# Four tiles instead of three for each part of the divided weights

## The chip, the cores and the metric

The kernel runs on one core of one Trainium2 chip. The metric is the device time of one execution in microseconds (us), lower is better.

## The reference

The reference is one block of a trunk on x of 512 tokens by 1024 features, float32 throughout. With u = rms_norm(x):

```
fa, fb, fc, fd, fg = split(u @ w_in)
branches = rwkv7_mix(fa), gla_mix(fb), mlstm_mix(fc), ssd_mix(fd)      # each [512, 512]
gates    = sigmoid(fg)                                                # four of [512, 1024]
merged   = sum_i gates[i] * (branches[i] @ branch_proj[i])
h = x + merged @ w_out
gate, val = split(causal_dwconv(rms_norm(h) @ ffn_up, 3 taps))        # 2 x 2816
h = h + (silu(gate) * val) @ ffn_down
return rms_norm(h)
```

The four mixers are recurrences over the tokens (RWKV7, gated linear attention, mLSTM, state space), computed here in chunks. `ssd_mix` matters below. For each of four blocks of 128 tokens and each of eight heads it forms exp(min(a_t - a_s, 0)) under a causal mask, multiplies it by the product of C and B, and applies that 128 by 128 matrix to the values.

## The kernel before, in words

**The dense work.** Every large matrix is read from memory in halves of 128 by 512 floats (256 KB). `split_h` (lines 220 to 228) handles one half: SP issues the load into a `raw` tile (line 222, three of them), ACT rounds it into `hi` (line 225), and DVE, or POOL for some, writes the rest, raw - hi, into `lo` (line 226). Both come from `w_tiles` (lines 217 and 218), a ring of three tiles for `hi` and three for `lo`. A product is then three matmuls (`mm3`, lines 234 to 237): hi by hi, lo by hi, hi by lo. A half feeds 12 matmuls in `fm` (512 tokens wide, called wide below) and 24 in `tm` and `fm_halves` (256 wide, called narrow below). A `hi` tile is free again when the last matmul that reads it is done; the next cast into it waits for that.

**The branches** interleave with it. The RWKV part runs in two halves. Each half solves a triangular system by 62 dependent instructions on DVE (lines 600 and 602 in turns), sends the result out and back by DMA, and goes on at line 629; its last matmuls are at lines 728 and 736. `conv4` (line 907 three times, line 910) and the GLA preparation (line 805) work on finished dense products and so free their PSUM banks, of which the dense products have three.

**The state space part** (`ssd`, named the SSD stage below: from the first half's line 728 to the last of lines 1056 and 1062). For each block b = 0 to 3: SP broadcasts a row of decays into a `sab` tile of 512 KB (line 1019, two tiles, so the third transfer waits for the matmuls of the first block), DVE and POOL take half of the subtractions each (line 1041, eight per block), ACT takes the exponential (line 1042), POOL applies the mask (line 1043), DVE multiplies by the product (line 1052), and PE applies the result (line 1056). POOL has small steps between these (lines 1039, 1057, 1064, 1073).

**The tail.** After the last branch come w_out, the norm, and the up projection. Its first two columns (`first`, line 1239) run by halves of tokens. For the second of these columns the second half of the weights has two tiles of its own, `wxh` and `wxl`, from a pool that lives until line 1240. The FFN loop (lines 1268 to 1273) and the down projection follow; line 1265 is their convolution.

**What sets the order.** The program is written once, and a scheduler of the framework then orders the instructions of every engine by a simulated timeline, with priorities from a table of numbers. Each engine runs its list strictly in order. The number of tiles in a ring is an input to that simulation.

Of the kernel before, what the change touches and what calls it, by code (L numbers as in the profile page):

```python
# [10 lines left out]
F32R = mybir.dt.float32r  # L11
# [5 lines left out]
P = 128  # L17
# [143 lines left out]
def kernel(ctx: ExitStack, tc: tile.TileContext, A, out):  # L161
# [25 lines left out]
    wp = ctx.enter_context(tc.tile_pool(name="wp", bufs=1))  # L187
# [7 lines left out]
    def pd():  # L195
        return dense[0].tile([P, T], F32, tag="d", name="psd")
# [18 lines left out]
        return pf[lo:hi, PF_AT[name] + i:PF_AT[name] + i + 1]  # L215

    def w_tiles():
        return (wp.tile([P, 512], F32R, tag="hi", name="hi", bufs=3), wp.tile([P, 512], F32R, tag="lo", name="lo", bufs=3))

    def split_h(src, h, tiles=None, eng=V):  # L220
        raw = wp.tile([P, 512], F32, tag="raw", name="raw", bufs=NRAW)
        nc.sync.dma_start(raw, src[:, 512 * h:512 * h + 512])
        hi, lo = tiles or w_tiles()
        with tc.high_priority(Q["split"]):
            S.copy(hi, raw)  # L225
            eng.tensor_tensor(lo, raw, hi.bitcast(F32), op=ALU.subtract)  # L226
        return hi, lo
# [3 lines left out]
    def split_w(src, tiles=(None, None), eng=V):  # L231
        return [split_h(src, h, tiles[h], G if (pl[0] >> h) & 1 else eng) for h in range(2)]

    def mm3(ps, lh, ll, rh, rl, first, last):
        PE.matmul(ps, lh, rh, start=first, stop=False)  # L235
        PE.matmul(ps, lh, rl, start=False, stop=False)  # L236
        PE.matmul(ps, ll, rh, start=False, stop=last)  # L237
# [36 lines left out]
    def fm_halves(jobs, eng=V):  # L274
        ws = [split_w(src, tiles, eng) for src, tiles in jobs]
        pss = [pd() for _ in jobs]
        for h in range(2):
            ts = slice(256 * h, 256 * h + 256)
            for w, ps in zip(ws, pss):
                for k in range(KD):  # L280
                    hi, lo = w[k // 4]
                    ks = slice((k % 4) * P, (k % 4 + 1) * P)
                    mm3(ps[:, ts], hi[:, ks], lo[:, ks], uh[:, k, ts], ul[:, k, ts], k == 0, k == KD - 1)
        return pss
# [924 lines left out]
    nc.sync.dma_start(gb2, A["gvec"][D:2 * D].partition_broadcast(P))  # L1209
    gb3 = hp.tile([P, D], F32, name="gb3")  # L1210
    nc.sync.dma_start(gb3, A["gvec"][2 * D:3 * D].partition_broadcast(P))
    hw_ctx = ExitStack()
    hw = hw_ctx.enter_context(tc.tile_pool(name="hw", bufs=1, side="right", reuse_waits="tile"))
    wx = [hw.tile([P, 512], F32R, name=n) for n in ("wxh", "wxl")]
    hx = ExitStack()
    np_ = hx.enter_context(tc.tile_pool(name="nq", bufs=1, side="right", reuse_waits="tile"))

# [18 lines left out]
        norm_T(h2[:, b], gb2, b, np_, uh, ul, 1, [pr_, pm])  # L1236
    tap("h2", h2)
    hx.close()
    first = fm_halves([(A["up"][0], (None, None)), (A["up"][1], (None, (wx[0], wx[1])))])
    hw_ctx.close()  # L1240
    wo_ctx.close()
    mo_ctx.close()
    ps_ctx.close()
# [91 lines left out]
```

## Time and profile before

| | |
|---|---|
| median of 3 runs | 1195.45 us (1193.54 to 1199.78) |
| the profiled execution | 1195.54 us |
| its span, first to last instruction | 1193.7 us |
| mean granted TensorE clock | 0.984 |
| busy PE / DVE / ACT / POOL | 1143.7 / 651.6 / 444.4 / 331.4 us |
| chain that ended last | PE 74%, DVE 11%, DMA 7%, issue 4% |

The profiled execution is 1.8 us longer than its span and 0.1 us above the median. The busy time of PE counts overlapping matmuls once. The chain is followed back from the last instruction to whatever released each step.

### The profile page before, as it was taken

How to read it: one execution, taken by the hardware profiler on the slowest of the kernel's cores; microseconds unless marked ns; L12 is line 12 of the kernel's file. 1: busy time of each engine (PE TensorE's matmuls, PEld its weight loads, DVE VectorE, ACT ScalarE, POOL GpSimd, SP SyncE). 2: the span in 40 equal slices, each digit the busy share in tenths (PEclk: the TensorE clock that was granted, in tenths of full speed). 3: DMA queues.
4: the chain of work that ended last, by engine and by line, in shares of the span. 5: the costliest groups of instructions: out<-in, count | busy, mean ns of one | idle time of the engine just before them, and what ended most of it. 6: DMA issues, size and time to landing. Idle time of an engine off the chain costs nothing.

```text
span 1193.7 us, 17895 instructions
## 1 busy us (share of the span) xinstructions
PE 1143.7 (96%) x6881; PEld 928.9 (78%) x6881; DVE 651.6 (55%) x1090; ACT 444.4 (37%) x820; POOL 331.4 (28%) x287
## 2 busy tenths in 40 slices
PE   5999989999999999989999999999999999999997
PEld 4887868777788767778777777778788888888886
DVE  5258796453576365793235653554665666652323
ACT  4355234332333432232124343432444444442323
POOL 3104012230285543331114543620212222220100
PEclk9999989999998999999999999999999999999999
DMA  5222322322341322332224523561232223222322
GB/s 198 65 98 64 88 61 70 103 78 79 105 98 53 98 80 67 93 83 91 68 84 150 160 88 115 184 201 38 89 101 96 96 96 99 97 97 97 97 97 107
DMA packets 79886, 117.30 MB, mean 98 GB/s; under 512 B 22660, under 2 KB 27172, under 8 KB 79800
## 3 DMA queue, kind: packets, MB, share of 16 engines
q1 hardware_dynamic: 79224, 115.11, 30.6%
q8 instruction: 54, 0.88, 0.3%
q10 hardware_dynamic: 576, 1.05, 0.2%
q14 instruction: 32, 0.26, 0.1%
HBM read 107.93 MB, written 8.19 MB: 97 GB/s over the span
## 4 chain that ended last, share of the span: by engine, by line
PE 74%; DVE 11%; DMA 7%; issue 4%; ACT 2%; POOL 1%; SPq 1%; POOLq 0%; DVEq 0%; ACTq 0%
PE psd L235 17%; PE psd L236 16%; PE psd L237 16%; PE psd L1282 3%; PE psd L1283 3%; PE psd L1284 3%; DVE Mi L602 2%; DVE Mt L600 2%; DMA sab<-ad 2%; DVE lo L226 1%; PE psr L676 1%; PE psd L331 1%; PE psd L330 1%; DMA raw<-in_wo_dram 1%; PE psd L332 1%
## 5 line engine op out<-in xcount | busy, mean ns | idle before, releaser
L226 DVE TENSOR_TENSOR lo<-raw,hi 128x512 fp32r<-128x512 f32 x280 | 229.0, 819 | 312.0 <-ACT hi L225 300.6
L225 ACT CAST hi<-raw 128x512 fp32r<-128x512 f32 x322 | 199.6, 620 | 485.7 <-PE psd L236 300.9
L235 PE MATMUL psd<-uh,hi 128*128 128x512 f32 (+1 forms) x912 | 359.9, 395 | 11.5 <-DVE w L907 4.8
L237 PE MATMUL psd<-uh,lo 128*128 128x512 f32 (+1 forms) x912 | 357.6, 393 | 4.5 <-DVE lo L226 4.1
L236 PE MATMUL psd<-ul,hi 128*128 128x512 f32 (+1 forms) x912 | 356.2, 391 | 0.2 <-DVE ul L252 0.2
L235 PEld LDWEIGHTS psd<-uh,hi 128*128 128x128 f32 x912 | 172.2, 189 | 53.0 <-ACT hi L225 6.2
L237 PEld LDWEIGHTS psd<-uh,lo 128*128 128x128 f32 x912 | 172.2, 189 | 44.8 <-DVE lo L226 5.6
L236 PEld LDWEIGHTS psd<-ul,hi 128*128 128x128 f32 x912 | 172.3, 189 | 36.8 <-issue 2.6
L226 POOL TENSOR_TENSOR lo<-raw,hi 128x512 fp32r<-128x512 f32 x42 | 56.9, 1356 | 194.2 <-ACT hi L225 157.5
L1271 POOL TENSOR_TENSOR y<-y 128x512 f32<-128x512 f32 x22 | 28.3, 1288 | 174.0 <-DVE y L1265 160.1
L1265 DVE SCALAR_TENSOR_TENSOR y<-psd,pf,y 128x510 f32<-128x510 f32 x88 | 65.9, 750 | 2.7
L1284 PE MATMUL psd<-hi,al 128*128 128x512 f32 x164 | 63.8, 389 | 0.0
L1283 PE MATMUL psd<-lo,ah 128*128 128x512 f32 x164 | 63.8, 389 | 0.0
L331 PE MATMUL psd<-lo,uh 128*128 128x256 f32 x192 | 57.1, 298 | 1.0 <-DVE lo L226 1.0
L1282 PE MATMUL psd<-hi,ah 128*128 128x512 f32 x164 | 57.3, 389 | 0.0
L332 PE MATMUL psd<-hi,ul 128*128 128x256 f32 x192 | 56.3, 294 | 0.0
L330 PE MATMUL psd<-hi,uh 128*128 128x256 f32 x192 | 55.8, 292 | 0.0
L331 PEld LDWEIGHTS psd<-lo,uh 128*128 128x128 f32 x192 | 37.8, 197 | 5.2 <-issue 3.3
L332 PEld LDWEIGHTS psd<-hi,ul 128*128 128x128 f32 x192 | 37.9, 197 | 1.3 <-issue 1.0
L330 PEld LDWEIGHTS psd<-hi,uh 128*128 128x128 f32 x192 | 37.7, 197 | 1.6 <-issue 1.2
L1284 PEld LDWEIGHTS psd<-hi,al 128*128 128x128 f32 x164 | 30.8, 188 | 6.5
L1282 PEld LDWEIGHTS psd<-hi,ah 128*128 128x128 f32 x164 | 30.8, 188 | 6.4
(418 smaller groups left out, 1696.5 us busy)
## 6 DMA issues: line engine op xcount, KB each, us to landing
raw<-in_wfm_dram SPq DMA_DIRECT2D x140, 256.0 KB, 2.6
raw<-in_up_dram SPq DMA_DIRECT2D x88, 256.0 KB, 2.5
raw<-in_dn_dram SPq DMA_DIRECT2D x44, 256.0 KB, 2.5
raw<-in_bp_dram SPq DMA_DIRECT2D x32, 256.0 KB, 2.7
raw<-in_wtm_dram SPq DMA_DIRECT2D x24, 256.0 KB, 2.6
raw<-in_wo_dram SPq DMA_DIRECT2D x16, 256.0 KB, 3.0
gd<-th SPq DMA_DIRECT2D x15, 256.0 KB, 2.1
th<-gd SPq DMA_DIRECT2D x15, 256.0 KB, 2.9
```

The source lines that it names most:

```text
L225: S.copy(hi, raw)
L226: eng.tensor_tensor(lo, raw, hi.bitcast(F32), op=ALU.subtract)
L235: PE.matmul(ps, lh, rh, start=first, stop=False)
L236: PE.matmul(ps, lh, rl, start=False, stop=False)
L237: PE.matmul(ps, ll, rh, start=False, stop=last)
L330: PE.matmul(o, uh[:, k, bs], hi[:, cs], start=first, stop=False)
L331: PE.matmul(o, uh[:, k, bs], lo[:, cs], start=False, stop=False)
L332: PE.matmul(o, ul[:, k, bs], hi[:, cs], start=False, stop=last)
L1265: V.scalar_tensor_tensor(y[:, d:T], ps[:, 0:T - d], col("fcw", k * 44 + n), y[:, d:T], op0=ALU.mult, op1=ALU.add)
L1282: PE.matmul(ps, ah[:, k, bs], hi, start=(k == 0), stop=False)
L1283: PE.matmul(ps, ah[:, k, bs], lo, start=False, stop=False)
L1284: PE.matmul(ps, al[:, k, bs], hi, start=False, stop=(k == NF - 1))
```

## The change

The rings of `hi` and of `lo` get a fourth tile. The pool with `wxh` and `wxl` goes, and the half that used it takes tiles of the rings like all others. Nothing else is edited.

```diff
     def w_tiles():
-        return (wp.tile([P, 512], F32R, tag="hi", name="hi", bufs=3), wp.tile([P, 512], F32R, tag="lo", name="lo", bufs=3))
+        return (wp.tile([P, 512], F32R, tag="hi", name="hi", bufs=4), wp.tile([P, 512], F32R, tag="lo", name="lo", bufs=4))
...
-    hw_ctx = ExitStack()
-    hw = hw_ctx.enter_context(tc.tile_pool(name="hw", bufs=1, side="right", reuse_waits="tile"))
-    wx = [hw.tile([P, 512], F32R, name=n) for n in ("wxh", "wxl")]
...
-    first = fm_halves([(A["up"][0], (None, None)), (A["up"][1], (None, (wx[0], wx[1])))])
-    hw_ctx.close()
+    first = fm_halves([(A["up"][0], (None, None)), (A["up"][1], (None, None))])
```

The lists of all engines come out in another order from about 70 us on. Three places follow; the rows are instructions in the order of their engine, with the number of equal neighbours behind.

PE in the SSD stage, before, at the matmuls of block 1 (line 1056, reading `sab`); L330 to L332 and L237 are dense matmuls, L1031, L1048, L1049 prepare later blocks, L1062 and L1068 handle the state:

```order
L330 MATMUL psd<-hi,uh 128x256 x2
L237 MATMUL psd<-ohg,lo 128x512
L1056 MATMUL psm<-w,sab 128x64 x8
L1062 MATMUL psm<-w 128x256 x2
L1068 MATMUL psr<-w,sbt 128x256 x2
L1031 MATMUL psr<-cst,w 128x128 x4
L1048 MATMUL psr<-w 128x128 x2
L331 MATMUL psd<-lo,uh 128x256
L332 MATMUL psd<-hi,ul 128x256
```

PE at the matmuls of blocks 0 and 1, changed:

```order
L332 MATMUL psd<-hi,ul 128x256
L1056 MATMUL psm<-w,sab 128x64 x4
L1068 MATMUL psm<-w,sbt 128x256 x2
L1056 MATMUL psm<-w,sab 128x64 x4
L1049 MATMUL psr<-cst,w 128x128 x2
L1056 MATMUL psm<-w,sab 128x64 x8
L1062 MATMUL psm<-w 128x256 x2
L1068 MATMUL psr<-w,sbt 128x256 x2
L1031 MATMUL psr<-cst,w 128x128 x4
L1048 MATMUL psr<-w 128x128 x2
L1049 MATMUL psm<-cst,w 128x128 x2
```

Before, 32 narrow matmuls and one wide one stood between the line 1056 of block 0 and that of block 1, and 41 narrow ones between blocks 1 and 2. Now blocks 0 and 1 stand together, then come 23 narrow ones and block 2. In all, the stage held 70 wide and 132 narrow dense matmuls before, and holds 16 and 133 now; 68 wide and 50 narrow more stand ahead of its beginning.

POOL in the same stage, before, from the subtractions of block 2:

```order
L1041 TENSOR_SCALAR sab<-sab,stk 128x128 x4
L1064 TENSOR_TENSOR w<-w 128x512
L1043 TENSOR_TENSOR sab<-sab,cst 128x1024
L1039 TENSOR_TENSOR w<-w,sf 128x512
L1073 TENSOR_TENSOR w<-w,sf 128x512
L1041 TENSOR_SCALAR sab<-sab,stk 128x128 x4
L1057 TENSOR_TENSOR w<-w,dskip 128x512
L1043 TENSOR_TENSOR sab<-sab,cst 128x1024
```

POOL there, changed:

```order
L1041 TENSOR_SCALAR sab<-sab,stk 128x128 x4
L1064 TENSOR_TENSOR w<-w 128x512
L1039 TENSOR_TENSOR w<-w,sf 128x512
L1073 TENSOR_TENSOR w<-w,sf 128x512
L1041 TENSOR_SCALAR sab<-sab,stk 128x128 x4
L1043 TENSOR_TENSOR sab<-sab,cst 128x1024
L1057 TENSOR_TENSOR w<-w,dskip 128x512
L1039 TENSOR_TENSOR w<-w,sf 128x512
L1043 TENSOR_TENSOR sab<-sab,cst 128x1024
```

The mask of block 2 (line 1043, the first of the two) stood right behind the subtractions of block 2 and line 1064. It now stands behind those of block 3 too. In the queue of SP the transfers of `sab` for blocks 2 and 3 (line 1019) now follow each other, where three weight loads stood between.

DVE at the end of the first solve, before (line 603 follows the last of the 62):

```order
L602 TENSOR_TENSOR Mi<-Mi,Mt 64x3x29
L832 SCALAR_TENSOR_TENSOR w<-w,gdk 128x128
L600 TENSOR_TENSOR Mt<-Ls,Mi 64x60
L602 TENSOR_TENSOR Mi<-Mi,Mt 64x2x30
L600 TENSOR_TENSOR Mt<-Ls,Mi 64x31
L602 TENSOR_TENSOR Mi<-Mi,Mt 64x31
L603 COPY Ls<-Mi 64x1024
L805 SCALAR_TENSOR_TENSOR qz<-psd,w 64x16x32 x2
L907 SCALAR_TENSOR_TENSOR w<-psd,pf,w 128x509
L907 SCALAR_TENSOR_TENSOR w<-psd,pf,w 128x510
```

DVE there, changed:

```order
L602 TENSOR_TENSOR Mi<-Mi,Mt 64x4x28
L799 COPY gdk<-w 128x16
L805 SCALAR_TENSOR_TENSOR qz<-psd,w 64x16x32 x2
L910 SCALAR_TENSOR_TENSOR w<-w 128x512
L600 TENSOR_TENSOR Mt<-Ls,Mi 64x87
L602 TENSOR_TENSOR Mi<-Mi,Mt 64x3x29
L600 TENSOR_TENSOR Mt<-Ls,Mi 64x60
L602 TENSOR_TENSOR Mi<-Mi,Mt 64x2x30
L600 TENSOR_TENSOR Mt<-Ls,Mi 64x31
L602 TENSOR_TENSOR Mi<-Mi,Mt 64x31
L603 COPY Ls<-Mi 64x1024
```

The two instructions of line 805 moved from behind the solve into it. Line 910, of which one is seen here, gains one inside the solve, and line 907 three. From its first to its last instruction DVE has 106 where it had 99; in the second solve 78 where it had 74, there too three more of line 907 and one of line 910. On PE, 25 more wide matmuls stand between the last matmul that prepares the first solve (line 576) and line 629.

## Rows read from the trace of the kernel before

**Rows 1.** the page, section 1: busy us (share) xinstructions of engines
```profile
PE 1143.7 (96%) x6881; PEld 928.9 (78%) x6881; DVE 651.6 (55%) x1090; ACT 444.4 (37%) x820; POOL 331.4 (28%) x287
```

**Rows 2.** stretches: length, busy of PE, PEld, DVE, ACT, POOL, PEclk, DMA share, GB/s
```profile
150.00:175.00 25.00, 19.64 (x190) 16.25 (x189) 24.61 (x57) 9.53 (x18) 5.16 (x4) 0.86 0.18 54
...
315.00:375.00 60.00, 55.68 (x352) 49.39 (x350) 40.42 (x82) 16.57 (x38) 41.84 (x34) 0.94 0.33 88
...
475.00:545.00 70.00, 64.06 (x436) 51.15 (x435) 55.45 (x98) 22.36 (x39) 24.99 (x23) 0.97 0.34 95
...
840.00:1180.00 340.00, 340.00 (x1502) 281.55 (x1501) 172.32 (x217) 133.62 (x218) 62.65 (x48) 1.00 0.29 95
...
355.00:365.00 10.00, 6.76 (x39) 6.47 (x38) 5.41 (x12) 2.26 (x5) 9.71 (x9) 0.73 0.18 48
```

**Rows 3.** waits: engine and line <- releaser: idle us, times, mean
```profile
ACT hi L225 <- PE psd L236: 300.9, 174, 6.2
```

**Rows 4.** groups by form: xcount, busy us, mean ns, idle before <-releasers
```profile
L235 PE MATMUL psd<-uh,hi 128*128 128x512 f32 x888 | 353.2, 398 | 11.3 <-DVE w L907 4.8 <-ACT hi L225 3.3 <-DVE y L1265 1.5
...
L237 PE MATMUL psd<-uh,lo 128*128 128x512 f32 x888 | 350.9, 396 | 4.5 <-DVE lo L226 4.1 <-POOL lo L226 0.4
```

**Rows 5.** SSD stage, timeline of PE: start us, us, ... [idle before <-releaser]
```profile
315.14 0.60 PE L728 MATMUL psr<-cst,Yt 128*128 128x128 f32 x4
...
339.96 1.22 PE L1056 MATMUL psm<-w,sab 128*128 128x64 f32 x10
...
355.23 0.28 PE L332 MATMUL psd<-hi,ul 128*128 128x256 f32 x1
...
357.14 0.28 PE L330 MATMUL psd<-hi,uh 128*128 128x256 f32 x1
...
360.66 0.69 PE L1056 MATMUL psm<-w,sab 128*128 128x64 f32 x2 [3.24 <-DVE sab L1052]
...
374.95 0.36 PE L330 MATMUL psd<-hi,uh 128*128 128x256 f32 x1
```

**Rows 6.** SSD stage, timeline of POOL
```profile
335.34 5.20 POOL L1043 TENSOR_TENSOR sab<-sab,cst 128x1024 f32<-128x1024 f32 x2
...
348.28 3.98 POOL L1041 TENSOR_SCALAR sab<-sab,stk 128x128 f32<-128x128 f32 x4 [1.01 <-ACT sf L1026]
...
352.35 1.29 POOL L1064 TENSOR_TENSOR w<-w 128x512 f32<-128x512 f32 x1
...
353.61 2.37 POOL L1043 TENSOR_TENSOR sab<-sab,cst 128x1024 f32<-128x1024 f32 x1
...
356.95 1.04 POOL L1073 TENSOR_TENSOR w<-w,sf 128x512 f32<-128x512 f32 x1
...
358.27 3.11 POOL L1041 TENSOR_SCALAR sab<-sab,stk 128x128 f32<-128x128 f32 x4 [0.28 <-ACT sf L1026]
```

**Rows 7.** SSD stage, timeline of DVE, and of the queue of SP
```profile
336.01 2.28 DVE L226 TENSOR_TENSOR lo<-raw,hi 128x512 fp32r<-128x512 f32 x1 [2.22 <-ACT hi L225]
...
357.01 0.99 DVE L1025 TENSOR_TENSOR sf<-sab,stk 128x8 f32<-128x8 f32 x1 [3.34 <-DMA sab<-ad]
...
359.93 1.27 DVE L1052 SCALAR_TENSOR_TENSOR sab<-psr,sab 128x512 f32<-128x512 f32 x2
...
341.92 0.38 SPq L1019 DMA_DIRECT2D sab<-ad  x1
```

**Rows 8.** the first solve: PE timeline, and the durations of DVE line 907
```profile
158.72 0.80 PE L235 MATMUL psd<-uh,hi 128*128 128x512 f32 x1 [4.78 <-DVE w L907]
...
L907 DVE SCALAR_TENSOR_TENSOR w<-psd,pf,w x36: 728/748/751, 155.8 to 544.4; 128x509 f32<-128x509 f32 x12, 128x510 f32<-128x510 f32 x12, 128x511 f32<-128x511 f32 x12
```

**Rows 9.** groups of PE, stretch 425 to 475, then 475 to 545 us
```profile
L235 PE MATMUL psd<-uh,hi 128*128 128x512 f32 x31 | 12.8, 414 | 1.8 <-ACT hi L225 1.8
...
L237 PE MATMUL psd<-uh,lo 128*128 128x512 f32 x61 | 24.8, 407 | 3.8 <-DVE lo L226 3.3 <-POOL lo L226 0.4
```

**Rows 10.** timeline of PE where the up projection begins
```profile
837.98 0.47 PE L235 MATMUL psd<-uh,hi 128*128 128x512 f32 x1 [1.49 <-DVE y L1265]
```

## Prediction

> **What bounds the kernel now.** I read the page first: PE is busy for 1143.7 us of the span [rows 1], so time can only come from the places where PE waits or runs slowly. The stretches show where those are. From 840 to 1180 us PE is full: 1502 matmuls in 340 us, one each 0.226 us [rows 2]. That is the price of a wide matmul. A narrow one costs 0.119 us: 16 steps from 355.23 to 357.14 us [rows 5]. No fourth tile can help that stretch. The first solve (150 to 175), the SSD stage (315 to 375) and the second solve (475 to 545) lose 5.4, 4.3 and 5.9 us to idle PE [rows 2].
>
> Next the waits. ACT stands idle before its casts for 300.9 us, waiting for matmuls [rows 3]. This is the row that invites the change: the cast has its data and waits for a tile. But it is idle time of an engine that is ahead. What PE itself waits for shows in its groups. Before a wide matmul on hi it lost 3.3 us to late casts, before one on lo 4.1 us to DVE and 0.4 us to POOL [rows 4]: 7.8 us in all. That is what the tiles can win directly, 0.7% of the time.
>
> **The change, part by part.** The work of PE is the same; its order is not. So each stage is costed by what it holds and by the chain that sets its end.
>
> *SSD stage.* It takes 59.8 us, from line 728 at 315.14 to the next dense matmul at 374.95 [rows 5]. Its chain does not depend on the dense work: transfer, subtractions, mask, product, and only then line 1056. The dense matmuls between the steps are cover. The changed list takes 54 wide ones out and puts one narrow in: 54 x 0.226 - 0.1 = 12.1 us less cover. They stand before line 728 and behind the stage now, where PE has no hole for them to fill. If the stage could shrink by 12.1 us, nothing would change. I count the chain from line 728:
> - Block 0. PE reached its line 1056 after 24.8 us [rows 5]. With 67 wide fewer and 76 narrow more ahead of it, it arrives at 24.8 - 15.1 + 9.0 = 18.7 us. The data are later: the first of two masks ends at 335.34 + 2.6 = 337.94 [rows 6], the product adds 1.3 us [rows 7], so 24.1 us. Before, they were hidden behind the dense work; now PE waits 5.4 us.
> - Block 2. Its transfer was issued 2.0 us after line 1056 of block 0 began, at 341.92 [rows 7], and its subtractions on POOL began 6.4 us later [rows 6]. From 24.1 us that gives 32.5 us. Then POOL in its new order: subtractions 4.0, line 1064 1.3, two steps of 1.0, the subtractions of block 3 3.1, the mask 2.4 [rows 6], then the product 1.3 us on DVE: 46.6 us. Before, line 1056 of block 2 ran at 360.66 [rows 5], after 45.5 us.
> - From there to the end took 14.3 us with 41 narrow matmuls [rows 5], 4.9 us. Now 14 wide and 16 narrow stand there, 5.1 us. The end is at 46.6 + 14.5 = 61.1 us.
>
> So the stage gets 1.3 us longer while it holds 12.1 us less: 13.4 us lost. I take off 0.9 us, since block 2's subtractions on POOL may take the 3.1 us that block 3's took rather than 4.0 [rows 6]. **+12.5 us.** [...] The lower end is +4: no such loss (-2.7), all four subtractions of both blocks at their fastest (-1.7), and a chain that starts some 4 us earlier against line 728. The last is an estimate, more than half of the 6.4 us of a transfer, for the scan and the first transfer hang on no matmul of line 728. The upper end is +16: the same clock loss once more after block 0.
>
> [...] Beside POOL's mask, one DVE subtraction for lo took 2.28 us [rows 7]. [...]
>
> *First solve.* DVE has seven instructions more inside it, at 0.75 us as line 907's [rows 8]: +5.2 us until its result leaves, and line 629 waits for that. PE does 25 wide matmuls more meanwhile, 5.7 us, where it had waited 4.78 us for line 907 to free a bank [rows 8]. Since what is done there need not be done later, the net is -0.4 us. Ends: -5 when the wait goes and the added instructions fit into DVE's waits, +5 when PE runs out of tiles anyway.
>
> *Second solve.* Four instructions more on DVE, +3.0 us, and some 5 wide and 8 narrow matmuls more, 2.1 us: +0.9 us. The 3.8 us that PE lost there to late lo [rows 9] do not go. DVE was full through the solve, the end is set by the solve, and a lo that comes earlier only lets PE wait later.
>
> *Late weights elsewhere.* 7.8 less 3.8 leaves 4.0 us. The largest is 1.8 us before a cast between 425 and 475 us [rows 9]. There ACT was late with the cast, and one half more in store is 12 matmuls, 2.7 us: enough. I take all of it, **-4.0 us**; the ends are 0 and -7, the latter with the 2.7 us that the clock lost after the longer wait above.
>
> *The up projection.* The half that had its own tiles now takes ring tiles, freed by the last matmul of `first`. A wait of 1.49 us stands there already [rows 10]; one lo subtraction of 0.75 us now stands between two convolutions on DVE, so +0.6 us. Ends 0 and +2.3.
>
> The sum is 12.5 - 0.4 + 0.9 - 4.0 + 0.6 = +9.6 us on the profiled 1195.5 us, which is 0.1 us above the median. I forecast **1205 us**.
>
> **The rivals.**
> *Faster.* The extra tile does what the ACT row promises. All 7.8 us of late weights go, the first solve gives 5 us, and the SSD chain starts 3 us earlier and loses only 4: 1195.5 - 7.8 - 5 + 4 + 1.5 (the second solve and the up projection) = 1188 us. For it: these waits are real. Against it: half of them are DVE's in the solve, and POOL's order in the SSD stage is fixed. It decides at line 1056 of block 2: ready 59.8 - 12.1 - 14.5 = 33 us after line 728 it loses nothing, at 46.6 us it loses all 13.4. [...]
>
> *Nothing to measure.* A fourth hi without a fourth raw holds one half more, and PE was late for few. The SSD stage loses 4 to 6, the weights give 4, the rest cancels: 1195 to 1198 us. For it: PE is full for 96%. Against it: 12.1 us of cover are gone from a stage whose chain is known.
>
> *Slower still.* The SSD stage loses 16, the solves 5, and no late weight is won: 1195.5 + 16 + 5 + 1.5 = 1218 us. Its price is the clock falling after both waits.
>
> **How the numbers follow.** A measurement of this kernel can tell about 0.5% from no change, 6 us: 1189.5 to 1201.4. My forecast of 1205 with its near neighbours gets 0.47, faster 0.17, nothing 0.29, slower still 0.07. Faster lies mostly under 1189.5 us; nothing lies in the band; the other two lie above it, with 0.02 of the forecast's own spread reaching into the band. That gives 0.17, 0.31 and 0.52. The range of 1187 to 1214 us takes in the faster case, the bounds of the SSD term with the others at their middle, and leaves out the extremes.
>
> **What would show it.** Right: PE in the SSD stage waits some 5 us at line 1056 of block 0 and 10 or more at that of block 2, both for DVE's line 1052, and POOL is nearly without gaps between; the stage takes 58 us or more with 149 dense matmuls; the granted clock falls behind both waits. The casts' wait on hi between 425 and 475 is gone. The first solve ends 5 us later against its beginning, with no wait for line 907. Wrong: line 1056 of block 2 starts under 40 us after line 728, or late lo in the second solve fall from 3.8 us to under 1 us and line 629 comes no later.

## The result, and the profile after

| | before | changed |
|---|---|---|
| median | 1194.49 us (1192.93 to 1199.78, 4 runs) | 1229.72 us (1226.94 to 1230.95, 4 runs) |
| the profiled execution | 1195.54 us | 1230.95 us |
| its span | 1193.7 us | 1229.2 us |
| mean granted clock | 0.984 | 0.970 |

The ratio is 1.0284, with a 95% interval from 1.0246 to 1.0321. The forecast was slower, at 1205 us; it is 1230 us, outside the range of 1187 to 1214.

The page of the changed kernel, section 1, against [rows 1]:

```profile
PE 1157.5 (94%) x6881; PEld 939.7 (76%) x6881; DVE 650.4 (53%) x1090; ACT 446.0 (36%) x820; POOL 332.5 (27%) x287
```

The work is the same to the matmul. PE idles 1229.2 - 1157.5 = 71.7 us where it idled 50.0, 21.7 us more; and the same 6881 matmuls keep it busy 13.8 us longer, with the mean granted clock down from 0.984 to 0.970. The 21.7 and the 13.8 us make the 35.5 us of the span. As an estimate from the two clocks, 0.030 x 1229.2 - 0.016 x 1193.7 = 17.8 us more of full speed were lost, part of it while PE waited (from 390 to 392 us PE is idle and the granted clock 0.50), so the clock is large enough for the 13.8 us.

The stretches of the changed kernel (columns as in [rows 2]; the SSD stage, then the stretch to the end of the second RWKV preparation, then the second solve; below, parts of the first two, and the up projection):

```profile
345.00:408.00 63.00, 48.18 (x298) 42.75 (x297) 38.37 (x81) 16.74 (x39) 43.29 (x36) 0.84 0.27 71
408.00:518.00 110.00, 97.26 (x509) 73.02 (x509) 47.89 (x73) 38.24 (x72) 44.88 (x35) 0.95 0.22 70
518.00:573.00 55.00, 49.58 (x225) 39.99 (x221) 47.38 (x89) 17.76 (x31) 22.68 (x17) 0.99 0.33 95
...
375.00:400.00 25.00, 16.01 (x75) 13.51 (x75) 17.10 (x33) 6.76 (x18) 20.84 (x18) 0.67 0.15 33
425.00:450.00 25.00, 15.68 (x64) 11.40 (x63) 7.39 (x14) 11.81 (x23) 11.41 (x9) 0.85 0.18 63
...
870.00:1210.00 340.00, 338.24 (x1485) 279.93 (x1486) 173.82 (x221) 136.22 (x221) 62.49 (x48) 0.99 0.29 96
```

The last row answers to the full stretch of [rows 2]: there next to nothing changed, PE idles 1.8 us. The SSD stage idles 14.8 us of 63, where its 60 us idled 4.3 [rows 2]; the stretch behind it idles 12.7 of 110 us, where the kernel before idles 2.5 of 105 (375 to 480, first row below). From 375 to 400 the granted clock is 0.67, and 0.50 in the part from 385 to 398. The kernel before from 375 to 480 us, then before and changed from 100 to 125 us, in the first RWKV preparation:

```profile
375.00:480.00 105.00, 102.53 (x569) 77.78 (x568) 53.91 (x81) 41.27 (x81) 46.81 (x36) 0.98 0.27 81
...
100.00:125.00 25.00, 24.91 (x227) 20.68 (x227) 18.41 (x33) 14.33 (x26) 7.49 (x8) 0.93 0.27 65
...
100.00:125.00 25.00, 22.92 (x155) 16.16 (x154) 14.20 (x24) 12.28 (x20) 6.61 (x7) 0.73 0.14 33
```

For each stage, "excess" below is how much longer it got, less the price of the dense matmuls that moved into it (plus that of those that moved out), at 0.226 and 0.12 us. The start is the first matmul, and each figure comes from one profiled execution of a kernel:

| stage | forecast, us | excess, us |
|---|---|---|
| start to the end of the first RWKV preparation | 0 | +7.3 |
| first solve, and on to line 728 | -0.4 | +1.1 |
| SSD stage | +12.5 | +15.3 |
| from there to the end of the second RWKV preparation | -4.0 | **+12.6** |
| second solve | +0.9 | -1.5 |
| from there to w_out | 0 | 0.0 |
| w_out, up projection, FFN loop | +0.6 | +0.4 |
| sum | +9.6 | +35.2 |

The groups of PE by form, against [rows 4], and the wait of ACT, against [rows 3]:

```profile
L235 PE MATMUL psd<-uh,hi 128*128 128x512 f32 x888 | 353.6, 400 | 18.7 <-DVE w L424 5.6 <-DVE w L907 4.0 <-DVE w L1085 3.4
...
L237 PE MATMUL psd<-uh,lo 128*128 128x512 f32 x888 | 351.8, 397 | 0.7 <-DVE lo L226 0.7
...
L330 PE MATMUL psd<-hi,uh 128*128 128x256 f32 x192 | 58.8, 306 | 6.6 <-DVE w L1085 4.6 <-DVE mg L411 2.0
```

```profile
ACT hi L225 <- PE psd L236: 326.2, 185, 6.0
```

The late weights are gone, as the change would have it: lo fell from 4.5 to 0.7 us, and no cast is among the first three releasers of line 235. In their place stand lines 424, 1085 and 411: DVE instructions that read a finished dense product and so free its PSUM bank. And ACT's wait before its casts, the row that invites the change, did not shrink but grew, from 300.9 to 326.2 us.

**The SSD stage.** PE from line 728 on (timeline of the changed kernel, against [rows 5]):

```profile
345.14 1.03 PE L728 MATMUL psr<-cst,Yt 128*128 128x128 f32 x8
...
357.38 0.71 PE L1048 MATMUL psr<-w 128*128 128x128 f32 x4 [1.32 <-DVE sbt L1050]
360.06 0.39 PE L330 MATMUL psd<-hi,uh 128*128 128x256 f32 x1 [1.97 <-DVE mg L411]
...
368.85 1.10 PE L1056 MATMUL psm<-w,sab 128*128 128x64 f32 x8 [1.29 <-DVE sab L1052]
...
392.72 0.58 PE L330 MATMUL psd<-hi,uh 128*128 128x256 f32 x1 [4.64 <-DVE w L1085]
...
397.79 2.10 PE L1056 MATMUL psm<-w,sab 128*128 128x64 f32 x16
...
407.35 0.87 PE L1062 MATMUL psr<-w 128*128 128x256 f32 x3
```

POOL in the same stage, from the subtractions of block 2 (against [rows 6]), and DVE:

```profile
378.40 3.06 POOL L1041 TENSOR_SCALAR sab<-sab,stk 128x128 f32<-128x128 f32 x4 [2.46 <-ACT sf L1026]
...
384.68 3.35 POOL L1041 TENSOR_SCALAR sab<-sab,stk 128x128 f32<-128x128 f32 x4
388.00 2.34 POOL L1043 TENSOR_TENSOR sab<-sab,cst 128x1024 f32<-128x1024 f32 x1
```

```profile
356.30 0.69 DVE L1038 TENSOR_TENSOR w<-w,sf 128x512 f32<-128x512 f32 x1
...
377.97 0.17 DVE L1025 TENSOR_TENSOR sf<-sab,stk 128x8 f32<-128x8 f32 x1 [4.00 <-DMA sab<-ad]
...
388.12 0.69 DVE L1033 COPY w<-psr 128x512 f32<-128x512 f32 x1 [1.21 <-PE psr L1031]
388.84 2.04 DVE L1038 TENSOR_TENSOR w<-w,sf 128x512 f32<-128x512 f32 x1
390.81 0.74 DVE L1085 SCALAR_TENSOR_TENSOR w<-w,psd 128x256 f32<-128x256 f32 x2
...
393.25 1.28 DVE L1052 SCALAR_TENSOR_TENSOR sab<-psr,sab 128x512 f32<-128x512 f32 x2
```

Block 0 reaches line 1056 after 23.7 us, the mask of block 2 ends after 45.2 us (388.00 + 2.34 - 345.14). The stage ends after 62.9 us and holds 16 wide and 133 narrow dense matmuls.

**The second RWKV preparation.** PE there:

```profile
431.59 0.50 PE L235 MATMUL psd<-uh,hi 128*128 128x512 f32 x1 [3.41 <-DVE w L1085]
...
440.93 1.88 PE L460 MATMUL psm<-w,cst 128*4 128x512 f32 x4 [0.27 <-ACT w L1106]
448.45 0.80 PE L235 MATMUL psd<-uh,hi 128*128 128x512 f32 x1 [5.64 <-DVE w L424]
...
457.97 0.55 PE L494 MATMUL psr<-cst,w 128*128 128x128 f32 x3 [1.95 <-DVE w L481]
```

The kernel before at the same lines:

```profile
400.44 1.02 PE L460 MATMUL psm<-w,cst 128*4 128x512 f32 x2
...
402.52 1.02 PE L460 MATMUL psm<-w,cst 128*4 128x512 f32 x2
...
419.06 0.49 PE L494 MATMUL psr<-cst,w 128*128 128x128 f32 x3
```

And DVE of the changed kernel:

```profile
447.57 0.32 DVE L466 TENSOR_SCALAR nn<-nn 128x16 f32<-128x16 f32 x1 [10.17 <-DMA nn<-nq]
447.65 0.74 DVE L424 SCALAR_TENSOR_TENSOR w<-psd,pf,w 128x511 f32<-128x511 f32 x1
455.85 0.75 DVE L524 SCALAR_TENSOR_TENSOR w<-w,pf 128x512 f32<-128x512 f32 x1 [7.45 <-DMA w<-nd]
456.52 0.74 DVE L424 SCALAR_TENSOR_TENSOR w<-psd,pf,w 128x511 f32<-128x511 f32 x1
457.18 0.74 DVE L481 SCALAR_TENSOR_TENSOR w<-psd,pf,w 128x511 f32<-128x511 f32 x1
```

Here lies a second chain like that of the SSD stage. Line 460 sums the squares of the keys; they go out by DMA (nq), come back (nn, line 466), go out and back again as scale factors (nd, line 524), and only then, in DVE's order, line 481 makes what line 494 transposes. From the last line 460 to line 494 that takes 15.75 us in the changed kernel and 16.12 us in the one before. But the one before has 68 wide matmuls in it, 15.4 us of cover, and the changed one 23, 5.2 us. It also starts late: ACT finished its input (line 459) at 418.76 us, and line 460 ran at 440.93, because PE's list has it behind the transposes of the SSD output (line 1104). In the kernel before, those were 3.1 us apart (397.3 and 400.4). Line 459 on ACT, before and changed:

```profile
396.60 0.73 ACT L459 ACTIVATE w<-w,pf 128x512 f32<-128x512 f32 x1
...
418.03 0.73 ACT L459 ACTIVATE w<-w,pf 128x512 f32<-128x512 f32 x1 [0.21 <-DVE w L424]
```

### The profile page after: what moved, and what is told of

Its sections match the earlier page's. It is cut to its first block, busy times and chain, and to the rows that moved or that the text cites. A ratio compares the mean times of both kernels' runs of the same rounds, so it can differ in the third digit from the quotient of the medians.

```text
span 1229.2 us, 17897 instructions
## 1 busy us (share of the span) xinstructions
PE 1157.5 (94%) x6881; PEld 939.7 (76%) x6881; DVE 650.4 (53%) x1090; ACT 446.0 (36%) x820; POOL 332.5 (27%) x287
## 5 line engine op out<-in xcount | busy, mean ns | idle before, releaser
L225 ACT CAST hi<-raw 128x512 fp32r<-128x512 f32 x323 | 200.5, 622 | 518.6 <-PE psd L236 326.2
L237 PE MATMUL psd<-uh,lo 128*128 128x512 f32 (+1 forms) x920 | 360.8, 393 | 0.7 <-DVE lo L226 0.7
L236 PE MATMUL psd<-ul,hi 128*128 128x512 f32 (+1 forms) x920 | 360.2, 393 | 0.2 <-DVE ul L252 0.2
L235 PEld LDWEIGHTS psd<-uh,hi 128*128 128x128 f32 x920 | 175.5, 191 | 59.6 <-issue 8.6
L237 PEld LDWEIGHTS psd<-uh,lo 128*128 128x128 f32 x920 | 175.4, 191 | 39.0 <-issue 1.8
L236 PEld LDWEIGHTS psd<-ul,hi 128*128 128x128 f32 x920 | 175.5, 191 | 37.3 <-issue 2.3
L330 PE MATMUL psd<-hi,uh 128*128 128x256 f32 x192 | 58.8, 306 | 6.6 <-DVE w L1085 4.6
L1278 PE MATMUL psd<-hi,ah 128*128 128x512 f32 x164 | 63.8, 389 | 0.0
L332 PE MATMUL psd<-hi,ul 128*128 128x256 f32 x192 | 59.1, 308 | 0.0
L330 PEld LDWEIGHTS psd<-hi,uh 128*128 128x128 f32 x192 | 39.8, 207 | 10.5 <-DVE w L1085 5.0
L332 PEld LDWEIGHTS psd<-hi,ul 128*128 128x128 f32 x192 | 39.8, 208 | 2.2 <-issue 1.8
L1279 PEld LDWEIGHTS psd<-lo,ah 128*128 128x128 f32 x164 | 30.8, 188 | 6.4
```

Of the source, the lines that this page charges most:

```text
L330: PE.matmul(o, uh[:, k, bs], hi[:, cs], start=first, stop=False)
L332: PE.matmul(o, ul[:, k, bs], hi[:, cs], start=False, stop=last)
L1278: PE.matmul(ps, ah[:, k, bs], hi, start=(k == 0), stop=False)
L1279: PE.matmul(ps, ah[:, k, bs], lo, start=False, stop=False)
```

## The experiments

Each kernel is compared with the one before in runs on the same chip; the dense counts and the excess of a stage are taken as above. The time of before in them is 1194.23, 1195.57, 1193.91 and 1194.99 us in the four groups of runs.

### Which of the tiles costs the time

**hi4_lo3**: four tiles for `hi` alone.

```diff
-        return (wp.tile([P, 512], F32R, tag="hi", name="hi", bufs=3), wp.tile([P, 512], F32R, tag="lo", name="lo", bufs=3))
+        return (wp.tile([P, 512], F32R, tag="hi", name="hi", bufs=4), wp.tile([P, 512], F32R, tag="lo", name="lo", bufs=3))
-    wx = [hw.tile([P, 512], F32R, name=n) for n in ("wxh", "wxl")]
+    wx = [hw.tile([P, 512], F32R, name=n) for n in ("wxl",)]
-    first = fm_halves([(A["up"][0], (None, None)), (A["up"][1], (None, (wx[0], wx[1])))])
+    first = fm_halves([(A["up"][0], (None, None)), (A["up"][1], (None, (wp.tile([P, 512], F32R, tag="hi", name="hi", bufs=4), wx[0])))])
```

> Four tiles for hi, three for lo; the half that had wxh and wxl takes a ring tile for hi and keeps wxl. Theory A (the fourth hi tile lets the scheduler put dense matmuls ahead of the stages whose chains they covered): the list holds 4 wide and 150 narrow dense matmuls in the SSD stage (18.9 us, the changed kernel 19.6, before 31.7), so the SSD stage loses 12 to 18 us against before and the time is 1210 to 1235 us. Theory B (the loss comes from the fourth lo tile, or from taking wxl away): 1190 to 1200 us.

Measured: 1219.52 us, ratio 1.0214 (1.0174 to 1.0253). The SSD stage has 4 wide and 150 narrow dense matmuls and an excess of 9.4 us, where 12 to 18 were expected; PE waits for line 1052, as the forecast has it for the changed kernel:

```profile
380.31 1.97 PE L1056 MATMUL psm<-w,sab 128*128 128x64 f32 x8 [4.25 <-DVE sab L1052]
```

**hi3_lo4**: the mirror image, four for `lo` alone, `wxh` kept.

```diff
-        return (wp.tile([P, 512], F32R, tag="hi", name="hi", bufs=3), wp.tile([P, 512], F32R, tag="lo", name="lo", bufs=3))
+        return (wp.tile([P, 512], F32R, tag="hi", name="hi", bufs=3), wp.tile([P, 512], F32R, tag="lo", name="lo", bufs=4))
-    wx = [hw.tile([P, 512], F32R, name=n) for n in ("wxh", "wxl")]
+    wx = [hw.tile([P, 512], F32R, name=n) for n in ("wxh",)]
-    first = fm_halves([(A["up"][0], (None, None)), (A["up"][1], (None, (wx[0], wx[1])))])
+    first = fm_halves([(A["up"][0], (None, None)), (A["up"][1], (None, (wx[0], wp.tile([P, 512], F32R, tag="lo", name="lo", bufs=4))))])
```

> Three tiles for hi, four for lo; wxh stays. The list keeps the dense matmuls of every stage within 1 of before, though hundreds of neighbours on PE change places. Theory A: no stage loses cover, 1188 to 1197 us, and the waits for late lo (4.5 us before) are smaller or the same. Theory B: 1210 us or more. Theory C (the table of priorities is fitted to one order, and any other order costs tens of microseconds): 1205 us or more.

Measured: 1196.92 us, ratio 1.0024 (1.0001 to 1.0047). The SSD stage holds 70 wide and 131 narrow matmuls, 70 and 132 before.

**raw4**: four tiles for the loads, three for both parts.

```diff
-NRAW = 3
+NRAW = 4
```

> The kernel before with four raw tiles: one more load ahead of the casts, the same three hi and lo tiles, the same dense matmuls in every stage. Theory A: 1190 to 1197 us, since a deeper store of loads does not move matmuls. A rival of it, that the depth of the store of weights as such makes the scheduler run ahead: 1210 us or more. Theory C: 1205 us or more.

Measured: 1196.00 us, ratio 1.0018 (0.9998 to 1.0038).

The loss comes with the fourth `hi`: 25 of the 35 us with it alone, 2 to 3 us with a fourth `lo`, 2 with a fourth `raw` (neither is far from the noise), and these last two leave the SSD stage its 70 wide and 131 or 132 narrow matmuls. With a fourth `hi` the scheduler places dense matmuls earlier, and they are missing in the SSD stage. The 25 us do not lie where the 35 do: in hi4_lo3 the second preparation has an excess of 1.5 us, and about 9 us lie behind the second solve. What makes these 9 us stays open. raw4, whose stages hold the same dense matmuls as before, shows how far a stage of one execution strays: its excesses go from -2.8 to +1.9 us.

### Where in the program

In the next four, every fourth half takes a tile of its own tag (so ring of three and one more, the same store), in the whole program or in a part of it:

```diff
+    four, nw = [False], [0]
     def w_tiles():
-        return (wp.tile([P, 512], F32R, tag="hi", name="hi", bufs=3), wp.tile([P, 512], F32R, tag="lo", name="lo", bufs=3))
+        nw[0] += 1; x = four[0] and nw[0] % 4 == 0; return tuple(wp.tile([P, 512], F32R, tag=n + "x" * x, name=n, bufs=1 if x else 3) for n in ("hi", "lo"))
...
-    pl[0] = Q["L_p1"]
+    four[0] = True; pl[0] = Q["L_p1"]
```

The last two lines are those of late4; the others set the flag in the same way at other lines. `first` takes these tiles too, and the pool `hw` is gone. The flag `four` is set from the start (**all4_cut**), from the second RWKV preparation on (**late4**), from the GLA part to the values of the SSD part (**only_gla**), or from the branch behind it, with the z product, to the second RWKV preparation (**only_br1**); the last two set it again at `first`.

> The same store as in the changed kernel, built in another way: rings of three and one tile that every fourth half takes, in the whole program. The scheduler makes another list of it: the SSD stage holds 29.1 us of dense work, the stretch behind it 71.4 (changed 70.6, before 77.9). Theory A, cover by itself: the SSD loss is under 4 us, the stretch behind loses some, 1200 to 1212 us. If the store as such costs: 1222 us or more, as the changed kernel.

> The fourth hi and lo tile exists from the second RWKV preparation on (every fourth half takes it), and the first three quarters of the branches run with three. The list holds the same dense matmuls as before in every stage up to the end of the SSD stage (31.7 us in it). Theory E (the loss is the dense work that the scheduler pulls forward while the chains of the GLA and SSD parts are still to come; where no such chain follows, a fourth tile costs nothing): 1186 to 1196 us, with no loss in the SSD stage and in the stretch behind it. Theory F (a fourth tile costs everywhere, or the removal of wxh and wxl does): 1200 us or more.

> The fourth tile exists only for the weights of the GLA part (and the first up projection). The SSD stage holds its 31.7 us as before; 18 wide matmuls more stand in the first solve and 18 fewer behind it. Theory E: a loss at the first solve and the RWKV steps behind it, 3 to 12 us in all, none in the SSD stage: 1197 to 1207 us. Theory F: 1194 to 1198 us.

> The fourth tile exists only for the weights of branch 1 and of the z part of the state space mixer, the dense work that covers the SSD stage, and for the first up projection. The list up to there is the one of before; 70 wide matmuls move ahead of line 728, the SSD stage holds 23.9 us of dense work (31.7 before, 19.6 in the changed kernel). Theory E: this alone brings back most of the loss of the SSD stage and of the stretch behind it (28 us in the changed kernel): 1207 to 1225 us. Theory F: 1195 to 1203 us.

| kernel | us | ratio (95%) | what its stages show |
|---|---|---|---|
| all4_cut | 1214.16 | 1.0162 (1.0126 to 1.0199) | SSD +9.7, first preparation +5.6, second +5.3 |
| late4 | 1194.33 | 1.0003 (0.9985 to 1.0020) | as before up to the end of the SSD stage; second preparation -1.7, second solve +0.5 |
| only_gla | 1205.68 | 1.0087 (1.0057 to 1.0118) | SSD +1.0, first solve (to line 629) +1.6, w_out and behind it +5.2 |
| only_br1 | 1206.04 | 1.0097 (1.0071 to 1.0123) | 70 wide and 11 narrow more ahead of line 728; SSD +9.8, second preparation +3.6 |

only_br1 repeats the forecast step by itself: the dense work of the branch, let loose ahead of line 728, costs 9.8 us in the SSD stage. late4 tests the other side, the gain. Where the fourth tile comes after the SSD stage, it costs nothing and brings nothing. Three of the four expectations failed in part. only_br1 was to cost 13 us or more and costs 12: its two excesses are 13.4 us, half of what the changed kernel loses in these two stages. only_gla came out inside its range, but by luck: the loss was expected at the first solve, and most of it lies from w_out on. all4_cut keeps 29 of the 31.7 us of dense work in the SSD stage and was to lose under 4 us there; it loses 9.7. So the amount of cover alone does not set the loss of that stage. The groups of late4, and its line 629 of the second solve:

```profile
L237 PE MATMUL psd<-uh,lo 128*128 128x512 f32 x888 | 350.8, 396 | 2.2 <-DVE lo L226 1.4 <-POOL lo L226 0.9
```

```profile
534.29 0.28 PE L629 MATMUL psr<-MN,zm 32*32 32x32 f32 x2 [4.31 <-DMA MN<-mnd]
```

Late lo fell from 4.5 to 2.2 us, and the wait for the solve's result, 0.6 us before, is 4.31: the stage takes 53.90 us, and took 53.85.

### The SSD stage: is it the cover, the subtractions, or the bank

**four_p1**: the changed kernel with another number in the scheduler's table, so that more dense work lies in the SSD stage.

```diff
-P_p1=60
+P_p1=120
```

> The changed kernel with the priority of the second RWKV preparation at 120 instead of 60: the SSD stage holds 28.0 us of dense work (changed 19.6, before 31.7), the stretch from there to the second solve 62.2 (changed 70.6, before 77.9). Theory A with cover as the only thing that counts: the SSD loss falls from 15 us to 5 to 8, the next stretch loses as much as now (13 us) or up to 8 more: 1218 to 1236 us. If the next stretch loses because of what stands in DVE's list rather than for want of dense work, it stays at 13 or less: 1215 to 1224 us.

Measured: 1226.58 us, ratio 1.0273 (1.0233 to 1.0313). The stage now holds 52 wide and 135 narrow matmuls, 8.4 us more than in the changed kernel, and its excess is still 15.1 us, where 5 to 8 were expected: it got 8.2 us longer. The 36 wide ones that were added run from 61.0 us after line 728 on, among the matmuls of line 1056 of the last block and of line 1062 behind it, and line 1056 of block 2 comes after 52.1 us, in the changed kernel after 52.7. Cover must stand inside the waits; behind them it only adds its own length.

**four_ah**: the changed kernel with all subtractions of line 1041 on DVE.

```diff
-E_ah=1
+E_ah=0
```

> The changed kernel with one number of its table changed: all eight subtractions of a block (line 1041) on DVE, none on POOL (E_ah 0 instead of 1). The SSD stage then holds only 2 wide and 94 narrow dense matmuls (11.7 us; changed 19.6). Theory A, cover by itself: 8 us less cover, the SSD stage loses more than the 15 us of the changed kernel, and the time is 1230 us or more. Theory D (the chain of the SSD stage is exposed because POOL's list puts the subtractions of block 3 ahead of the mask of block 2, and what frees PE's banks stands behind that chain in DVE's list): POOL's share of the chain falls by 3 to 4 us for each of two blocks, and the SSD loss goes from 15 to 8 us or less: 1207 to 1220 us. An estimate that walks the lists with the median durations of both traces gives 18 us less than the changed kernel.

Measured: 1219.48 us, ratio 1.0202 (1.0164 to 1.0239). POOL is relieved, and the stage's excess is 17.4 us, with 2 wide and 94 narrow matmuls; the wait is now behind DVE:

```profile
383.29 2.04 PE L1062 MATMUL psr<-w 128*128 128x256 f32 x4 [5.42 <-DVE w L1074]
```

So POOL's order, on which the forecast counted, is not the sole cause: without those subtractions the chain stands on DVE's list. The time lies in the range of theory D, whose reason, a loss of 8 us or less in this stage, did not hold. The 10 us that this kernel gains against the changed one lie elsewhere, in the second preparation (below).

**four_zc2**: the changed kernel with ACT copying the z product out of its PSUM bank, so that line 1085 holds none.

```diff
             S.activation(z, ps, AF.Tanh, scale=0.5)
-            V.scalar_tensor_tensor(z, z, 1.0, ps, op0=ALU.add, op1=ALU.mult)
+            zc = wp.tile([P, 256], F32, tag="zc", name="zc", bufs=2)
+            S.copy(zc, ps)
+            V.scalar_tensor_tensor(z, z, 1.0, zc, op0=ALU.add, op1=ALU.mult)
```

> The changed kernel, with ACT copying the finished z product out of its PSUM bank (two small tiles), so that DVE's line 1085 no longer holds the bank. The list of PE is the same until line 1056 of block 2 in the SSD stage, but for 8 narrow matmuls more ahead of it; behind the stage the new list puts 64 wide matmuls between line 460 and line 494 instead of 23. Theory: in the SSD stage the 4.64 us wait for line 1085 goes, but the chain still holds line 1056 of block 2 at 46 to 50 us after line 728, so PE waits there instead for 1 to 4 us: the stage's loss falls from 15.3 to 10 to 13 us. The second RWKV preparation, with 14.5 us of cover, loses 0 to 2 us instead of 12.6. Time 1212 to 1219 us. Rival (banks held by DVE are the whole loss of both stages): the SSD stage loses under 8 us, time 1203 to 1210 us. Second rival (the missing cover of line 460 is not the cause): the second preparation still loses 8 us or more, time above 1222 us.

Measured: 1214.85 us, ratio 1.0165 (1.0135 to 1.0196). In the SSD stage the 4.64 us wait for line 1085 is gone, and stands again at the next step:

```profile
390.54 3.67 PE L1056 MATMUL psm<-w,sab 128*128 128x64 f32 x16 [4.42 <-DVE sab L1052]
```

The stage's excess is 14.7 us; 10 to 13 were expected. The bank was in front of the chain and not the cause: 15.3 became 14.7. Which part of this stage's loss belongs to the missing cover and which to the order of POOL and DVE no run here separates: 11.7 us of dense work go with an excess of 17.4 (four_ah), 17.2 with 4.0 (four_best, below), 18.9 with 9.4 (hi4_lo3), 19.6 with 15.3 (changed) and 29.0 with 9.7 (all4_cut). The second preparation, with 64 wide matmuls in its chain again, has an excess of 0.7 us: that expectation held. Of the 15 us between this kernel and the changed one, 11.8 are there.

### The second preparation: the blocked bank, or the cover

**four_nn**: the changed kernel with line 466 issued on GpSimd. The lists of PE, ACT and SP stay the same to the instruction; on DVE, line 424 no longer stands behind a wait for DMA.

```diff
-        V.tensor_scalar(nn, nn, scalar1=1e-24, scalar2=None, op0=ALU.max)
+        G.tensor_scalar(nn, nn, scalar1=1e-24, scalar2=None, op0=ALU.max)
```

> The changed kernel with one instruction moved: the clamp of the RWKV norms (line 466), which waits for a transfer at the head of DVE's list, is issued on GpSimd. PE, ACT and SP keep their lists to the instruction, and on DVE line 424, which frees the PSUM bank that PE waits 5.64 us for, stands free. Theory (the chain is short of cover): from the last line 460 to line 494 the chain takes 15.75 us in the changed kernel and 16.12 in the one before, but holds 23 wide matmuls there (5.2 us) instead of 68 (15.4 us). Freeing the bank early only lets PE do its 23 matmuls early and then wait for line 481 at line 494. So the second RWKV preparation still loses 10 to 13 us and the time is 1228 to 1231 us. Rival (the blocked bank is the loss): the 5.64 us go, and some of the clock loss with them: 1221 to 1225 us, the stage loses 5 to 7 us.

Measured: 1231.76 us, ratio 1.0301 (1.0273 to 1.0329), 0.8 us above the range of the theory; the profiled execution is the slowest of four, 1236.59 us. Its PE:

```profile
448.42 0.80 PE L235 MATMUL psd<-uh,hi 128*128 128x512 f32 x1 [3.15 <-DVE w L424]
461.28 0.90 PE L494 MATMUL psr<-cst,w 128*128 128x128 f32 x3 [4.61 <-DVE w L481]
```

The bank came free earlier: 3.15 us of waiting instead of 5.64. Line 424 now waits for ACT instead, so the test takes away 2.5 us of the wait and not all of it:

```profile
447.62 0.75 DVE L424 SCALAR_TENSOR_TENSOR w<-psd,pf,w 128x511 f32<-128x511 f32 x1 [7.76 <-ACT w L423]
```

PE did its 23 matmuls, and then waited for line 481: 4.61 us instead of 1.95. The sum is 7.8 us against 7.6. From line 460 to line 494 it is 16.6 us. The excess of the stage is 14.6 us, above the 10 to 13 of the theory and far above the rival's 5 to 7. The blocked bank is where the loss shows, and the missing cover is what makes it. All kernels, ordered by the wide matmuls between the last line 460 and line 494:

| wide there | excess of the second preparation, us |
|---|---|
| 23 | 12.6 (changed), 12.2 (four_p1), 14.6 (four_nn) |
| 35 | 5.3 (all4_cut) |
| 45 to 50 | 4.0 (hi3_lo4), 1.5 (hi4_lo3), 3.6 (only_br1) |
| 64 to 68 | 0.7 (four_zc2), -1.7 (late4), -0.2 (three_gqk), 0 (before), 0.3 (raw4), 0.1 (only_gla), -1.5 (three_best) |
| 71 | -2.3 (four_ah), 0.3 (four_best) |

The chain itself takes 15.4 to 18.9 us in all of them.

### Other tables

A walk through neighbouring tables, in which each list was priced with durations of the traces, picked four numbers for the changed kernel (**four_best**); **three_best** has the same four with three tiles, and **three_gqk** is what the walk picked for three.

```diff
-L_go=1, E_b1=0, E_ah=1, WM=5
+L_go=0, E_b1=1, E_ah=0, WM=4
```

```diff
-P_gqk=1, P_m=60, E_xd=0
+P_gqk=200, P_m=0, E_xd=1
```

> Four tiles with the same four numbers (E_ah 0, E_b1 1, L_go 0, WM 4). The SSD stage holds 17.2 us of dense work, 2.4 us less than in the changed kernel. Theory A, cover by itself: 1220 us or more. Theory C: four tiles lose nothing once the list fits them, 1180 to 1196 us; the walk along the lists gives 10 us less than before.

> The kernel before (three tiles) with four numbers of its table changed: E_ah 0 (subtractions on DVE), E_b1 1 (one product of the second RWKV preparation on POOL), L_go 0 and WM 4 (which lo subtractions go to POOL, and which PSUM ring some steps use). Theory C (the table fits the list of one ring size, and numbers that fit four tiles don't fit three): 1197 to 1208 us; the same walk along the lists gives 7 us more than before. If these numbers are better by themselves: 1185 to 1192 us.

> Three tiles with three numbers changed that fit three better by the same walk (P_gqk 200, E_xd 1, P_m 0): 8 us less than before. If the walk is right to some 3 us, 1183 to 1191 us, and what four tiles give above three is the difference from the run with four. If the walk only sorts large differences: 1190 to 1200 us.

Measured: four_best 1202.47 us, ratio 1.0062 (1.0038 to 1.0086); three_best 1207.33 us, 1.0100 (1.0061 to 1.0139); three_gqk 1197.72 us, 1.0026 (1.0006 to 1.0046). The absolute forecasts of the walk missed: it sorts large differences and no small ones. But with these numbers four tiles are no slower than three (1202.47 us in six runs, 1207.33 in two; the intervals overlap, so that they are faster is not shown), and with the old ones 35 us slower. So the loss belongs to the list that comes out, not to the tile. In four_best the SSD stage takes 49.25 us with 8 wide and 128 narrow matmuls, an excess of 4.0, and the second preparation 0.3; what is left lies in the first preparation (+3.1) and the first solve up to line 629 (+4.3).

No kernel here beats the one before. Not tried: a table searched for four tiles by times from the chip, and four tiles of each beside `wxh` and `wxl`.

## Why the prediction was right and wrong

- **Same work, another order; each stage costed by what it holds and by its chain.** Right for most of the loss; of the 7.3 us at the start, up to 4.6 hang, as an estimate, on the clock of the one execution (below). The tail, where PE is full, moved by 0.4 us.
- **SSD stage, +12.5.** Right within its bounds of 4 to 16, at their upper end (12.5 and one more clock loss of 2.7 us are 15.2): 15.3. The 2.7 us, here, in the lower end of +4 and in the end of -7 for the late weights, are an estimate from the 0.73 of [rows 2], 0.27 x 10 us; no run shows them as time by themselves. What the runs showed is the granted clock of 0.67 from 375 to 400 us, by the same estimate 0.33 x 25 = 8.3 us of full speed, a part of it while PE was idle. Block 0 was forecast after 24.1 us and came after 23.7; POOL began the subtractions of block 2 after 33.3 us (378.40), forecast 32.5; the mask of block 2 was forecast to end at 45.3 (46.6 less the product) and ended at 45.2. Two steps behind that were not counted. On DVE the product of block 2 stands behind lines 1038, 1085 and 1095 and began 2.9 us after the mask. And PE stood at a dense matmul for a bank that line 1085 freed late, then did 23 narrow ones, 0.21 us apart at a granted clock of 0.50 where 0.12 is their price, and came to line 1056 at 52.7 instead of 46.6 us. So the waits forecast at line 1056 itself, 5 and 10 us, stood mostly ahead of it, at lines 1048 and 330 and at small steps between. From there to the end it took 10.3 us instead of 14.5. These two misses, +6.1 and -4.2 us, partly cancel, and that the number came so close is to that extent luck. The lower end, in which the chain starts earlier against line 728, did not come about: line 1025 of block 0 ran 11.0 us after line 728, 10.7 before.
- **Late weights elsewhere, -4.0: the step that failed.** Measured +12.6; of the 25.6 us between the forecast sum and the measured one, 16.6 lie here and 7.3 at the start. The waits for weights went, as forecast (4.5 to 0.7 at lo, no cast among the first three releasers at hi). The error was to cost the stretch from 375 to 480 us by these waits alone. It holds a chain of its own, line 460 to line 494, some 16 us, and that lost 45 of its 68 wide matmuls, 10.2 us of cover. PE idles 10.2 us more in the stretch, 12.7 after 2.5, and its granted clock there is 0.95 after 0.98. The lists show the missing 45 ahead of time, just as they show the 54 of the SSD stage. With this term at +10, and the wait of line 235 for line 1085 (3.41 us) left out, the forecast would have been 1219 us. four_nn and four_zc2 tell this cause from the blocked bank.
- **First solve, -0.4.** The solve took 5.3 us longer, from its first instruction to the one that sends it off (42.75 us before, 48.04 us after, by the start of line 603), forecast 5.2. The wait for line 907 did not go: 3.76 us after 4.78. Other matmuls moved in too. Up to line 629 the excess is +3.4; from there to line 728 it is -2.2, and the sum is +1.1.
- **Start to the first preparation, 0.** Measured +7.3, and not seen: the list of dense matmuls changes there from 70 us on, in its order and not in its count. The matmuls at line 568 wait 2.02 us for DVE, and one at line 549 1.68 us for POOL, where it was 0.40. Most of the rest goes with the clock: from 100 to 125 us it is 0.73, and 0.93 before, as an estimate 0.20 x 25 = 5.0 us of full speed. In four_p1 and four_zc2, with the same list of PE up to there, the excess is 2.7 us, in four_nn 8.7. In four_p1 too the clock falls, to 0.86 from 100 to 125 us. So some 3 us come with this order in all four executions, and 0 to 6 more in one; that these go with the clock is an estimate from the changed kernel and four_p1. What decides them stays open.
- **Second solve, +0.9.** Measured -1.5. The reason held: the late lo went, and line 629 waits 4.54 us for the result (0.62 before). late4 shows the same by itself.
- **Up projection, +0.6.** Measured +0.4; the wait of [rows 10] is 2.07 us after 1.49. The step from a subtraction of 0.75 us to 0.6 us has no row behind it, and a stage of one execution strays by more than this.
- **POOL's steps and ACT's waits.** POOL's four subtractions took 3.06 us for block 2, 3.98 before, as the 0.9 us taken off has it, but 3.35 for block 3, 3.11 before, and the mask 2.34 after 2.37. The chain gained nothing by it, since DVE and PE stood later. The repeated gaps that invite the change were those of ACT, which is not the engine that should be full: with more tiles ACT's 174 waits became 185, and the time grew by 2.8%.
- **The rivals.** The faster one named its test, line 1056 of block 2 at 33 or 46.6 us; it came at 52.7. The slower one, 1218 us, had the sign of the missing terms, but put them down to the clock and the solves.

## What to carry to other kernels

In a list that a scheduler fixes from a simulation, a deeper buffer can move work between stages more than it shortens waits: here it lost 35 us where 7.8 us of waits were to be won. Go through every chain of fixed length (a round trip by DMA, a solve, a scan), not only the one next to the edit: count the work of the bounding engine that stands inside its waits before and after, and price the difference. A wait for a PSUM bank on an engine's list can be only where such a shortage shows, as in four_zc2 (4.64 us, then 4.42 at the next step) and four_nn (5.64 and 1.95 us, then 3.15 and 4.61); free the bank and see whether the wait moves on.

## What the runs showed of the hardware that was not expected

- Some of what DVE does beside POOL's mask takes longer: line 1038 takes 0.69 us at 356.30 us, and 2.04 us beside the mask of 388.00. Line 1033, a copy out of PSUM, takes 0.69 us beside the same mask. The mask itself took 2.34 us, 2.37 before, so the cost was on DVE's side of the chain here.
- PE was busy 13.8 of the 35.5 us longer with the same matmuls, without any wait; that the granted clock (0.970 after 0.984) made them is the estimate above. Behind the waits of the SSD stage narrow matmuls start 0.21 us apart instead of 0.12, from 393.10 to 397.58 us, at a granted clock of 0.50.
